# Attention with a bias: scores in three PSUM places of two banks instead of two places of three

## The chip, the cores and the metric

The kernel runs on one core of one Trainium2 chip. The time is the device time of one execution in microseconds (us); shorter is better. A core has five engines that run side by side, each through its own list of instructions: TensorE (PE; its weight loads are shown apart as PEld), VectorE (DVE), ScalarE (ACT), GpSimd (POOL) and SyncE (SP, which only issues transfers here). PSUM, which PE writes its products to, has eight banks of 512 fp32 values for each of 128 partitions. "One bank" below means a block of 128 x 512 scores.

## The reference

```python
batch, n_heads, seq_len, head_dim = 4, 8, 1024, 64
scale = 1.0 / np.sqrt(head_dim)
scores = scale * np.matmul(q, k.transpose(0, 1, 3, 2)) + bias      # bias: 1 x 1 x 1024 x 1024
scores_max = np.max(scores, axis=-1, keepdims=True)
attn = np.exp(scores - scores_max) / (np.sum(np.exp(scores - scores_max), axis=-1, keepdims=True) + 1e-8)
return np.matmul(attn, v)
```

There are 32 heads. The scores of a head are 1024 x 1024: with 128 keys on the partitions that is 16 banks, 512 banks in all.

## The kernel before

**The computation.** Two heads make a pair, 16 pairs. Scores are computed transposed: keys on the partitions, queries along the columns, in eight blocks of 128 keys and eight chunks of 128 queries. ACT takes the exponential from PSUM into a ring `E` of bf16 banks in SBUF (`s_exp`, L204); no maximum is subtracted. A second product of exp(scores) with V, which has a column of ones beside its 64 (`av_blocks`, L265; four matmuls of 65 columns for each bank), collects output and sum for a unit; DVE takes the reciprocal of the sum (`rs`, L276), multiplies (`ob`, L277), and SP stores.

**Running differences.** The bias is added to a place in PSUM only once for a set of chunks. When the next head comes to the same place, its scores are not written anew. Instead one matmul over 128 rows adds the new head's product and subtracts the old one's, since K of both heads stands on the two halves of the rows (`KA` for the second head of a pair, `KB` for the first head with the pair before it) and Q stands beside it with signs (`QA`, `QB`). Bias plus scores is thus kept up to date in PSUM. A step that begins a set anew is a *restart*: it writes the bias (four matmuls with `btraw` a bank) and then the head's scores.

**The places.** Six PSUM banks hold scores, `XY` = two places `sx` and `sy` of three banks (L79). The other two, tags `xa` and `xb`, serve in turn for transpositions (`px`) and for the accumulators of units (`po`). The eight chunks are divided into sets: A (chunks 6 and 7), B (3 to 5) and C (0 to 2). In A each place holds one chunk in two banks, in B and C each holds half the key blocks of three chunks in three banks. A *slot* is one filling of a place: `s_fill(s)` writes it (L151), slots alternate between the places, and slot s may be filled when ACT has read slot s-2. There are 192.

**The order.** Groups of pairs (L83): pairs 0 to 3 run through A, B, C; 4 to 8 through C, A, B; 9 to 15 through B, C, A. A set that goes on from one group to the next is not restarted. Where A goes over into a three-bank set, the third bank is filled early (`pre_slots`, `pe_pre`). K and Q of a pair are loaded by POOL, transposed by PE (L140), and copied by DVE (L763, L770) and by SP's transfers into a ring of RP = 9 pairs.

**DVE's share.** DVE computes some banks' exponentials itself with seven instructions, a *chain*: `d_fixed` reads the bank (L216), `d_steps` are L228 to L233. `mark_next` chooses the last bank of a slot for it, if DVE's queue of chain work is at most REM.

**The planner.** When the kernel is built, a planner walks through an estimated time line and writes out the order of each engine's instructions: it holds estimated costs (`EXP`, `E2P`, ...), times at which data are there (`R`, `raw_at`, `v_ready`), and picks for PE among a fill, a transposition (`pe_piece`) and AV work (`pe_av`). A fill goes as soon as its place is free; other work is taken if it ends before the fill is due, or if more than RING = 38 banks of E wait for AV. Loads are paced by `gate`, in slots. `cut_of` says which slots' exponentials are cut in two, so that a place comes free bank by bank.

**The prologue** (L289 to L487) is written out by hand: the first six slots (0 to 5), pairs 0 and 1, with loads as fp32 into the unused end of E and casts by DVE, ACT and POOL.

**The end.** The last pair's unit is divided into its two heads (`units`, L237).

Of the kernel before, what the change touches and what calls it, by code (L numbers as in the profile page):

```python
# [8 lines left out]
F32 = mybir.dt.float32  # L9
# [7 lines left out]
def kernel(  # L17
# [25 lines left out]
    RP = 9  # L43
    EB = 56
# [39 lines left out]
    steps = []  # L84
    prev = None
    for prs, ps_order in groups:
        for pa in ps_order:
            for pr in prs:
                for h in range(2):
                    restart = pr == prs[0] and h == 0 and pa != prev  # L90
                    steps.append((pa, pr, h, restart))
            prev = pa
    first_of = {}
    for pa, pr, h, restart in steps:
        first_of[pa, pr] = restart or first_of.get((pa, pr), False)
    NSTEP = len(steps)
    NS = 2 * NSTEP
    first_step = {}
    last_step = {}
    for i, (pa, pr, h, r) in enumerate(steps):  # L100
        first_step.setdefault(pr, i)
        last_step[pr] = i

    def pieces_of(pa, y):

        c0, W = CH[pa]
        if W == 2:
            return [(kc, c0 + y, 1, kc * P) for kc in range(NCH)]
        out_ = []
        for kk in range(4):  # L110
            col, ci, n = kk * W * P, 0, W
            while n:
                m = min(n, 4 - col // P % 4)
                out_.append((4 * y + kk, c0 + ci, m, col))
                col, ci, n = col + m * P, ci + m, n - m
        return out_

    def blocks_of(pa, y):
        return [(kc, c + j, col + j * P) for kc, c, n, col in pieces_of(pa, y) for j in range(n)]

    def nbanks(pa):
        return CH[pa][1]
# [22 lines left out]
    pass_reads = {}  # L145
# [5 lines left out]
    def s_fill(s, banks, third=False):  # L151

        pa, pr, h, restart = steps[s // 2]
        ps_ = XY[s % 2]
        r = pr % RP
        ms = mm_of.setdefault(s, [])
        for b in banks:
            todo, bias_ = [], []
            for kc, c, n, col in pieces_of(pa, s % 2):
# [3 lines left out]
                o = ps_[:, col:col + n * P]  # L163
                if restart:

                    todo.append((o, (KB if pr else KA)[:, r, kcol], QB[:, r, qcol]))
                    for j in range(n):
                        t = btraw[:, c + j, :].rearrange("p (kp kc) -> p kc kp", kc=NCH)[:, kc, :]
                        bias_.append((ps_[:, col + j * P:col + j * P + P], t, ident8[:]))
# [5 lines left out]
            for i, (o, lhsT, rhs) in enumerate(todo):  # L175
                m = nc.tensor.matmul(o, lhsT, rhs, start=restart and i == 0, stop=i == len(todo) - 1 or not restart,  # L176
                                     skip_group_check=True)
                for lo, hi, x in pass_reads.get(s % 2, []) if third else reads_of.get(s - 2, []):
                    if not lo <= b < hi:
                        apart(m, x)  # L180
                ms.append((b, m))

    def read_of(s, lo, hi, inst):
# [7 lines left out]
        if steps[s // 2][0] == "A":  # L191
            pass_reads.setdefault(s % 2, []).append((lo, hi, inst))
            for s2 in (x for x in mm_of if x > s and x % 2 == s % 2):
                for b, m in mm_of[s2]:
                    if not lo <= b < hi:
                        apart(inst, m)
        else:
            pass_reads.pop(s % 2, None)
# [3 lines left out]
    def s_exp(s, lo, hi):  # L202
        at = (e_pos[s] + lo) * 512
        x = nc.scalar.activation(E[:, at:at + (hi - lo) * 512], XY[s % 2][:, lo * 512:hi * 512], ACTF.Exp, scale=scale)  # L204
# [10 lines left out]
    def d_fixed(ch, s, b):  # L215
        i = nc.vector.tensor_scalar(ys[ch % 2].bitcast(I32), XY[s % 2][:, b * 512:(b + 1) * 512],  # L216
# [21 lines left out]
    for i, (pa, pr, h, r) in enumerate(steps):  # L238
        if h == 0:
            units += [(pa, pr, i, [0, 1])] if i < NSTEP - 2 else [(pa, pr, i, [0]), (pa, pr, i, [1])]  # L240
    NU = len(units)
    po = {}
    left = {u: 2 * 4 * CH[x[0]][1] * len(x[3]) for u, x in enumerate(units)}
# [8 lines left out]
    def av_blocks(u, s, b, tag):  # L252
        pa, pr, i0, hs = units[u]
        h = s // 2 - i0
        c0, W = CH[pa]
# [5 lines left out]
        for kc, c, col in blocks_of(pa, s % 2):  # L261
# [7 lines left out]
    def evac(u):  # L269
        pa, pr, i0, hs = units[u]  # L270
        c0, W = CH[pa]
# [9 lines left out]
    with tc.manual_schedule():  # L281
# [33 lines left out]
        for prs, po_ in groups:  # L315
            for pa in po_:
                if first_of[pa, prs[0]]:
                    c0, W = CH[pa]
                    g.memset(QB[D:, prs[0] % RP, c0 * P:(c0 + W) * P], 0.0)
# [19 lines left out]

        cast(g, btraw[:, 6, 5 * P:], sc[6][:, 5 * P:])  # L340
        for pr in (2, 3):
            if pr == 3:
                cast(g, kr1[:, 1].rearrange("p c d -> p (c d)"), sk1[:, 512:])
                load_q(pr, 6, 8)
            x = g.dma_start(out=raws[pr, 1].rearrange("p t c d -> p t (c d)"), in_=kf[pr])
            if pr == 2:
                after(x, behind)
            if pr == 2:
# [669 lines left out]
```

## Time and profile before

| | us |
|---|---|
| median of three runs (239.46 to 239.92) | 239.59 |
| the profiled execution | 239.7 |
| its span, first to last instruction | 237.8 |
| ACT busy, 275 instructions | 225.6 |
| PE busy, 4010 matmuls | 224.2 |
| PE weight loads busy | 187.7 |
| DVE busy, 461 instructions | 220.8 |
| POOL busy | 57.5 |
| first exponential starts | 7.23 |
| last exponential ends | 232.44 |

The profile is of one execution on the chip. It lists each instruction with engine, line of the kernel, what it writes and reads ("E<-sx" writes E from sx), start and length. Busy time is time in which at least one instruction of the engine runs; matmuls are pipelined and their ends are modelled, so that a busy PE need not be a PE at its peak. Exponentials overlap with the one before by 0.1 to 0.2 us, so that the distance from start to start is their real cost.

### The profile page before, as it was taken

The page shows a single profiled execution, that of the slowest core. Times are in us where ns is not written, and L with a number is a line of the kernel's source. Part 1 is how long each engine was busy: PE and PEld are TensorE (multiplying, and loading weights), DVE is VectorE, ACT ScalarE, POOL GpSimd, SP SyncE. Part 2 cuts the span into 40 slices and gives each one's busy share as a digit, 9 for nine tenths or more (in the row PEclk, how much of TensorE's full clock was granted, in tenths as well). Part 3 has the DMA queues.
Part 4 walks back from the last instruction along what each step waited for, and adds up shares of the span by engine and source line. Part 5 has one row for each costly group of instructions (what it writes and reads, how often), then busy time and mean ns, then how long its engine had stood idle before and what let it go on. Part 6 is the DMA issues. An engine that isn't in the chain of part 4 may idle for free.

```text
span 237.8 us, 9441 instructions
## 1 busy us (share of the span) xinstructions
PE 224.2 (94%) x4010; PEld 187.7 (79%) x4010; DVE 220.8 (93%) x461; ACT 225.6 (95%) x275; POOL 57.5 (24%) x82
## 2 busy tenths in 40 slices
PE   7999899999999999999999999999998989989892
PEld 3778788887888889987777888888887777888782
DVE  3686999999989999999999999999999999999993
ACT  4799999999999999999999999999999999999991
POOL 5695502544112224633220332000000000000000
PEclk9999999999999999999999999999999999999999
DMA  7899999999999649999998899312121111111012
GB/s 231 224 136 182 177 195 222 178 189 193 221 211 158 116 93 197 158 183 160 207 209 234 144 135 147 88 44 68 36 69 36 36 34 36 36 55 36 25 48 66
DMA packets 60633, 30.98 MB, mean 130 GB/s; under 512 B 36016, under 2 KB 56624, under 8 KB 60592
## 3 DMA queue, kind: packets, MB, share of 16 engines
q0 software_dynamic: 42272, 13.50, 55.2%
q1 hardware_dynamic: 18176, 16.62, 24.9%
q8 instruction: 31, 0.51, 0.9%
q10 hardware_dynamic: 144, 0.26, 0.5%
q14 instruction: 10, 0.08, 0.1%
HBM read 29.36 MB, written 8.39 MB: 159 GB/s over the span
## 4 chain that ended last, share of the span: by engine, by line
DVE 49%; PE 34%; ACT 7%; issue 7%; DMA 2%; ACTq 0%; DVEq 0%
PE sx L176 9%; PE po L265 8%; PE sy L176 8%; ACT E L204 7%; DVE scr L216 7%; DVE scr L232 7%; DVE e L233 6%; DVE ob L277 6%; DVE scr L231 5%; DVE scr L230 4%; DVE scr L229 4%; PE px L140 4%; DVE scr L228 3%; DVE QA L770 2%; DVE rs L276 2%
## 5 line engine op out<-in xcount | busy, mean ns | idle before, releaser
L204 ACT ACTIVATE E<-sy 128x512 bf16<-128x512 f32 (+2 forms) x151 | 127.9, 906 | 0.2
L204 ACT ACTIVATE E<-sx 128x1024 bf16<-128x1024 f32 (+2 forms) x110 | 115.2, 1065 | 1.5 <-PE sx L176 0.9
L265 PE MATMUL po<-VV,E 128*128 128x65 bf16 x1888 | 84.2, 194 | 2.1 <-DVE ob L277 1.1
L265 PEld LDWEIGHTS <-E 128*128 128x128 bf16 x1888 | 76.0, 98 | 10.3 <-DVE ob L277 2.4
L176 PEld LDWEIGHTS <-KA 128*128 128x128 bf16 x648 | 47.3, 98 | 11.6 <-issue 3.5
L176 PEld LDWEIGHTS <-KB 128*128 128x128 bf16 x600 | 44.0, 98 | 11.7 <-issue 4.6
L134 POOL DMA_DIRECT2D VV<-in_v_dram x32 | 28.8, 905 | 40.9 <-ACT E L204 37.2
L176 PE MATMUL sx<-QA,KA 128*128 128x128 bf16 (+2 forms) x312 | 36.1, 252 | 1.9 <-ACT E L204 1.6
L176 PE MATMUL sx<-QB,KB 128*128 128x128 bf16 (+2 forms) x300 | 35.5, 251 | 2.4 <-ACT E L204 1.7
L176 PE MATMUL sy<-QA,KA 128*128 128x128 bf16 (+2 forms) x312 | 36.0, 252 | 0.4 <-ACT E L204 0.2
L176 PE MATMUL sy<-QB,KB 128*128 128x128 bf16 (+2 forms) x300 | 35.4, 251 | 0.8 <-ACT E L204 0.3
L233 DVE SCALAR_TENSOR_TENSOR e<-scr 128x512 bf16<-128x512 f32 x40 | 27.6, 690 | 1.1
L232 DVE SCALAR_TENSOR_TENSOR scr<-scr 128x512 f32<-128x512 f32 x40 | 27.4, 684 | 0.0
L230 DVE SCALAR_TENSOR_TENSOR scr<-scr 128x512 f32<-128x512 f32 x40 | 27.3, 684 | 0.0
L231 DVE SCALAR_TENSOR_TENSOR scr<-scr 128x512 f32<-128x512 f32 x40 | 27.3, 683 | 0.0
L277 DVE TENSOR_TENSOR ob<-po,rs 128x384 f32<-128x384 f32 (+2 forms) x49 | 24.8, 506 | 2.0 <-DMA out_dram<-ob 0.4
L216 DVE TENSOR_SCALAR scr<-sx 128x512 int32<-128x512 f32 x32 | 21.9, 684 | 1.7 <-ACT E L204 1.5
L131 POOL DMA_DIRECT2D kr<-in_k_dram x12 | 8.5, 705 | 42.2 <-ACT E L204 35.1
L229 DVE TENSOR_SCALAR scr<-scr 128x512 int16<-128x512 int16 x40 | 17.2, 429 | 0.0
L228 DVE TENSOR_SCALAR scr<-scr 128x512 f32<-128x512 uint16 x40 | 17.0, 425 | 0.2
L176 PEld LDWEIGHTS <-btraw 128*128 128x128 bf16 x128 | 11.3, 148 | 1.2 <-issue 0.5
L770 DVE TENSOR_SCALAR QA<-px,sgn 128x1024 bf16<-128x1024 bf16 (+2 forms) x18 | 12.0, 666 | 0.0
(79 smaller groups left out, 167.9 us busy)
## 6 DMA issues: line engine op xcount, KB each, us to landing
out_dram<-ob SPq DMA_DIRECT2D x32, 192.0 KB, 2.8
VV<-in_v_dram POOLq DMA_DIRECT2D x32, 128.0 KB, 7.4
kr<-in_k_dram POOLq DMA_DIRECT2D x14, 256.0 KB, 5.4
KB<-KA SPq DMA_DIRECT2D x24, 128.0 KB, 4.4
qr<-in_q_dram POOLq DMA_DIRECT2D x12, 256.0 KB, 6.7
QB<-qn SPq DMA_DIRECT2D x22, 128.0 KB, 5.8
out_dram<-ob SPq DMA_DIRECT2D x15, 128.0 KB, 4.7
btraw<-in_bias_dram POOLq DMA_DIRECT2D x2, 768.0 KB, 9.0
```

What stands on the lines that cost most here:

```text
L134: return [nc.gpsimd.dma_start(out=VV[:, pr % RP, t * NCH:(t + 1) * NCH, :D], in_=vf[pr][:, t].rearrange("p (c d) -> p c d", d=D)) for t in ...
L176: m = nc.tensor.matmul(o, lhsT, rhs, start=restart and i == 0, stop=i == len(todo) - 1 or not restart, skip_group_check=True)
L204: x = nc.scalar.activation(E[:, at:at + (hi - lo) * 512], XY[s % 2][:, lo * 512:hi * 512], ACTF.Exp, scale=scale)
L216: i = nc.vector.tensor_scalar(ys[ch % 2].bitcast(I32), XY[s % 2][:, b * 512:(b + 1) * 512], scale * LOG2E * 65536.0, 127.0 * 65536.0, op0= ...
L228: (340, lambda: v_.tensor_scalar(sf, lo, G / 65536.0, None, op0=ALU.mult)),
L229: (340, lambda: v_.tensor_scalar(sp, hi, 0.0, 128.0, op0=ALU.max, op1=ALU.mult)),
L230: (600, lambda: v_.scalar_tensor_tensor(sb, sf, U2, sf, op0=ALU.add, op1=ALU.mult)),
L231: (600, lambda: v_.scalar_tensor_tensor(y, sf, U1, sf, op0=ALU.add, op1=ALU.mult)),
L232: (600, lambda: v_.scalar_tensor_tensor(sb, sb, V2, sp.bitcast(BF), op0=ALU.add, op1=ALU.mult)),
L233: (650, lambda: v_.scalar_tensor_tensor(e[:], y, V1, sb, op0=ALU.add, op1=ALU.mult)),
L265: nc.tensor.matmul(po[u][:, h - hs[0], c - c0, :], e_block(s, col), VV[:, pr % RP, h * NCH + kc, :], start=first, stop=left[u] == 0, skip_ ...
L277: nc.vector.tensor_tensor(ob[:], acc[:, :, :, :D], rs[:].to_broadcast([P, nh, W, D]), op=ALU.mult)
```

## The change

Six banks are still used for scores, now as three places `z0`, `z1`, `z2` of two banks. Every slot has two banks, and there are 256. Slot s waits for the slot that last used its place, `was[s]`, in the steady part slot s-3.

In B and C the 24 blocks of a head (8 key blocks x 3 chunks) go over the three places in order, eight to each. Set A is divided into A0 (chunk 6) and A1 (chunk 7). For the first group the slots 0 to 15 use `z0` for A0 and `z1` for A1, and `z2` only in the prologue. In the later groups, now pairs 4 to 9 and 10 to 15, set A runs over three places (`pass_a`): of the twelve heads, `z0` and `z1` take A0 and A1 of the first eight, while `z2` takes A0 of the last four and then A1 of these.

A unit is now a pair with a range of chunks; where a pair's A0 and A1 run at different times (pairs 8, 9, 14, 15), each chunk is a unit of its own, and the last six slots are divided by head, the last three by chunk too. RP goes from 9 to 10, E from 56 to 50 banks, RING from 38 to 36, REM from 5000 to 3500. The early fill of a third bank is dropped, as are most cuts. `mark_next` may choose slots that follow each other, and always bank 1 of the next slot to be filled.

In the prologue the transposed K lies in `z2`; DVE copies both halves of KA (ACT did one); POOL casts pair 1's q (DVE did); the second half of K is copied by ACT and DVE (DVE alone did); pair 1's q is transposed earlier; K of pair 3 is loaded behind q of pair 3.

```diff
-    RP = 9
-    EB = 56
+    RP = 10
+    EB = 50
...
-    XY = [ps.tile([P, 3 * 512], F32, tag=t, name=t) for t in ("sx", "sy")]
-    CH = {"A": (6, 2), "B": (3, 3), "C": (0, 3)}
-    groups = [(range(0, 4), "ABC"), (range(4, 9), "CAB"), (range(9, NP), "BCA")]
+    Z = [ps.tile([P, 2 * 512], F32, tag=t, name=t) for t in ("z0", "z1", "z2")]
+    CH = {"A0": (6, 1), "A1": (7, 1), "B": (3, 3), "C": (0, 3)}
...
+        if W == 1:
+            return [(kc, c0, kc * P) for kc in range(NCH)]
+        return [(i // W, c0 + i % W, i % 8 * P) for i in range(8 * y, 8 * y + 8)]
...
+    slots = [(y, "A%d" % y, 0, pr, h) for pr in range(4) for h in range(2) for y in range(2)]
+    NA = len(slots)
+    def pass_(pa, prs):
+        return [(y, pa, y, pr, h) for pr in prs for h in range(2) for y in (2, 0, 1)]
+    def pass_a(prs):
+        hd = [(pr, h) for pr in prs for h in range(2)]
+        out_ = []
+        for i in range(8):
+            out_ += [(2, "A%d" % (i // 4), 0) + hd[8 + i % 4], (0, "A0", 0) + hd[i], (1, "A1", 0) + hd[i]]
+        return out_
+    g0, g1, g2 = range(4), range(4, 10), range(10, NP)
+    slots += pass_("B", g0) + pass_("C", g0) + pass_("C", g1) + pass_a(g1) + pass_("B", g1)
+    slots += pass_("B", g2) + pass_("C", g2) + pass_a(g2)
+    for s, (y, pa, yb, pr, h) in enumerate(slots):
+        was.append(at_.get(y))
+        at_[y] = s
+        b = slots[was[s]] if was[s] is not None else None
+        restart.append(b is None or b[1:3] != (pa, yb) or 2 * b[3] + b[4] + 1 != 2 * pr + h)
...
+    for s, (y, pa, yb, pr, h) in enumerate(slots):
+        joint = pa in "BC" or (pr - g1[0]) % 6 < 4 or pr < 4
+        hs, c = [0, 1], (CH[pa] if pa in "BC" or not joint else (6, 2))
+        if s >= NS - 6:
+            hs = [h]
+            if s >= NS - 3:
+                c = CH[pa]
...
+        cast(g, *q_part(1, 6, 8, sq1))
...
-        on(0, 2, 3, nc.scalar.copy(KA[:D, 0, :HK], pk[0][:D]))
-        on(1, 2, 3, v_.tensor_copy(KA[:D, 0, HK:], pk[1][:D]))
+        on(2, 0, 1, v_.tensor_copy(KA[:D, 0, :HK], pk[0][:D]))
         v_.tensor_copy(QB[:D, 0, 6 * P:], pq_[:D].rearrange("p c q -> p (c q)"))
+        on(2, 1, 2, v_.tensor_copy(KA[:D, 0, HK:], pk[1][:D]))
...
+        nc.scalar.copy(KA[D:, 0, :HK], pk0[0][D:])
+        v_.tensor_copy(KA[D:, 0, HK:], pk0[1][D:])
...
-        DMIN, DTAIL, DMAL, RING, PSL, PSU, URG, NEAR, REM = 14, 8, 5200, 38, 60, 150, 24, 3, 5000
-        G0, G1, G2, G3, G4, G5 = 18, 5, 12, 56, 6, 8
+        DMIN, DTAIL, DMAL, RING, PSL, PSU, URG, NEAR, REM = 14, 9, 5200, 36, 100, 200, 20, 3, 3500
+        G0, G1, G2, G3, G4, G5 = 20, 7, 16, 78, 10, 8
...
         def cut_of(s):
-            n = nbanks(steps[s // 2][0])
-            if s in mark or s < 6:
-                return None
-            if n == 3 and s // 2 + 1 in restarts:
-                return 2
-            if n == 2 and s % 2:
-                return 1
-            if s - 1 in mark or (n == 2 and s + 1 in mark):
-                return n - 1
-            return None
+            return s not in mark and (s < NA and s % 2 == 1 or s == NS - 1)
...
-            if s in pre_slots or s != len(fill_end) or not DMIN <= s < NS - DTAIL or s - 1 in mark or len(open_ch) >= 3 \
-                    or len(ch_run) >= 2 or ch_left[0] > REM:
+            if s != len(fill_end) or not DMIN <= s < NS - DTAIL or len(open_ch) >= 3 or len(ch_run) >= 2 or ch_left[0] > REM:
                 return
...
-            if s >= NS or s - 2 >= len(act_end) or (s - 2 in mark and len(read_end[s - 2]) < nbanks(steps[s // 2 - 1][0])):
+            if s >= NS or was[s] >= len(act_end) or (was[s] in mark and len(read_end[was[s]]) < 2):
                 return None
```

More of the change, by code (lines that the diff above doesn't have):

```diff
@@ L149, in apart, with s_fill @@
             tc.declare_no_dep(later.ins, earlier.ins, reason="different banks of one slot")
-    def s_fill(s, banks, third=False):
-        pa, pr, h, restart = steps[s // 2]
-        ps_ = XY[s % 2]
+    def s_fill(s):
+        y, pa, yb, pr, h = slots[s]
         r = pr % RP
         ms = mm_of.setdefault(s, [])
-        for b in banks:
+        for b in range(2):
             todo, bias_ = [], []
-            for kc, c, n, col in pieces_of(pa, s % 2):
+            for kc, c, n, col in pieces_of(pa, yb):
                 if col // 512 != b:
@@ L175, in s_fill @@
             for i, (o, lhsT, rhs) in enumerate(todo):
-                m = nc.tensor.matmul(o, lhsT, rhs, start=restart and i == 0, stop=i == len(todo) - 1 or not restart,
+                m = nc.tensor.matmul(o, lhsT, rhs, start=restart[s] and i == 0, stop=i == len(todo) - 1 or not restart[s],
                                      skip_group_check=True)
-                for lo, hi, x in pass_reads.get(s % 2, []) if third else reads_of.get(s - 2, []):
+                for lo, hi, x in reads_of.get(was[s], []):
                     if not lo <= b < hi:
@@ L510 @@
         next_load = next_v = 4
-        restarts = [i for i in range(1, NSTEP) if steps[i][3]]
-        pre_slots = []
-        for i in restarts:
-            if steps[i - 1][0] == "A":
-                pre_slots += [2 * i, 2 * i + 1]
-        pre_done = {}
         dve_q = []
@@ L695, in loads @@
             while next_v < NP and s > gate(next_v, 1) \
-                    and not any(units[u][1] == next_v - RP for u in range(av_u, NU)):
+                    and not any(units[u][0] == next_v - RP for u in range(av_u, NU)):
                 for x in load_v(next_v):
```

350 lines of the change are left out of this document (140 added, 210 removed).

## The prediction

> **What bounds the kernel now.** I read the page's parts 1 and 2, then busy time by stage, then ACT's own groups by form and its timeline, then PE's.
>
> ```profile
> span 237.8 us, 9441 instructions
> ...
> PE 224.2 (94%) x4010; PEld 187.7 (79%) x4010; DVE 220.8 (93%) x461; ACT 225.6 (95%) x275; POOL 57.5 (24%) x82
> ...
> PEclk9999999999999999999999999999999999999999
> ```
>
> Three engines lie within two per cent of each other and TensorE's clock is granted in full, so no single share of busy time decides. The windows say which engine is full in which stage (columns: length; then PE, PEld, DVE, ACT, POOL busy):
>
> ```profile
> 16.00:30.00 14.00, 12.54 (x202) 10.45 (x198) 12.01 (x26) 13.78 (x22) 8.69 (x11) 1.00 1.73 181
> 30.00:80.00 50.00, 49.79 (x924) 41.35 (x924) 48.36 (x98) 49.46 (x49) 16.20 (x21) 1.00 1.28 190
> 80.00:110.00 30.00, 29.34 (x602) 26.85 (x601) 29.38 (x62) 29.77 (x43) 12.78 (x17) 1.00 1.21 157
> 110.00:150.00 40.00, 39.99 (x727) 32.09 (x726) 39.24 (x81) 39.77 (x41) 8.47 (x10) 1.00 1.05 176
> 150.00:232.00 82.00, 76.42 (x1367) 65.57 (x1364) 80.80 (x166) 81.79 (x107) 0.00 (x0) 1.00 0.15 45
> ```
>
> ACT is busy 98 to 99.7% from 16 us to the last exponential. But its instructions overlap, so that column hides short waits; the starts show them:
>
> ```profile
> 24.38 0.75 ACT L204 ACTIVATE E<-sx 128x512 bf16<-128x512 f32 x1
> 24.86 0.77 ACT L204 ACTIVATE E<-sy 128x512 bf16<-128x512 f32 x1
> 25.33 1.21 ACT L204 ACTIVATE E<-sx 128x1024 bf16<-128x1024 f32 x1
> 26.24 1.22 ACT L204 ACTIVATE E<-sy 128x1024 bf16<-128x1024 f32 x1
> ...
> 35.27 1.47 ACT L204 ACTIVATE E<-sx 128x1536 bf16<-128x1536 f32 x1
> 36.66 1.45 ACT L204 ACTIVATE E<-sy 128x1536 bf16<-128x1536 f32 x1
> 38.01 1.45 ACT L204 ACTIVATE E<-sx 128x1536 bf16<-128x1536 f32 x1
> 39.34 1.03 ACT L204 ACTIVATE E<-sy 128x1024 bf16<-128x1024 f32 x1
> ```
>
> From start to start, the undisturbed steps (tenth percentile of all starts) are 0.476 us for one bank, 0.903 for two, 1.330 for three: 0.427 a bank and 0.049 an instruction. The trace has 122, 91 and 56 of these (the last has no follower): 121 x 0.476 + 91 x 0.903 + 56 x 1.330 = 214.3 us. From the first exponential (7.23) to the start of the last (231.75) are 224.5 us. Less one cast between them (1.0), that leaves **9.2 us in which ACT did not run at its rate**. By stage: 1.64 before 16 us, then 0.73, 2.06, 1.33, 1.31 and 2.19 in the five windows. Of these 0.92 are steps of 17 ns (0.920 for 0.903), the rest waits of 0.06 to 0.52 us.
>
> Can they go? That depends on PE. I give each matmul its median step: 29.5 ns for 65 columns, 55.5, 108.5 and 162 for 128, 256 and 384, 58 for a bias block, 36 for a transposition. What is then left of PE's time is 2.67 us in 30:80, of which 2.41 are the changes between transpositions and other matmuls (23 of some 0.1 us, none of them touched). In 110:150 it is 2.51, with 2.52 such. So **PE is full in 30:80 and 110:150** and ACT's 3.37 us there are mostly PE's. In 80:110 PE has 2.3 us beside these changes, in 150:232 about 12. Counting exponentials against the 65-column matmuls that use them (four a bank), 30 to 38 banks wait for AV from 50 to 75 us, 10 at 90, 39 at 135, 2 to 3 from 165 on: work is put off up to the limit RING=38 in both full stretches.
>
> **The change, part by part.** The sum is made against the profiled execution, 239.7 us (span 237.8 and 1.9 around it); the median of the three runs, 239.59, is 0.1 lower.
>
> 1. *Three places.* A fill may start once the exponential three slots back is done, no longer two back. Before, with 128x1536, a fill has 1.33 us of the other place's exponential for 0.66 of matmuls and the hand-overs; after it has 2 x 0.90 for 0.45. What goes: in 80:110 the 1.33 less 0.15 of small steps, 1.18; in 150:232 2.19 - 0.28 = 1.91 (the larger waits there, 1.0 us in sum, sit where DVE reads its bank late, 209.4 to 212.5 and near 220; one place more covers such a reading); in 110:150 only the waits before 130 us, when AV can still be put off, 0.49; in 30:80 no more than the 0.26 that PE has left; in 16:30 0.15, as its 0.52 at 29.1 is PE waiting for DVE's copies (L773). Together **-4.0**. The lower end is 0 (a later wait takes each place), the upper 6.7 (all that are not small steps).
> 2. *Form of the exponentials.* 256 slots of two banks. With 40 DVE banks as now: 206 x 0.903 + 60 x 0.476 (40 marked; 20 from the ten slots cut in two) = 214.6, against 214.3: **+0.3**. Not fewer instructions: 266 against 269. But 206 two-bank steps stand where 91 were, and these show 0.903 and 0.920 about equally often, the three-bank ones nearly always 1.330: 115 x 0.008 = **+0.9**, between 0 and 2.6 (all at 0.920, less what is paid now).
> 3. *More restarts.* The third place restarts twice in each later two-chunk stage: 20 slots of two banks instead of 32 banks, so 32 bias matmuls more, 32 x 0.058 = 1.9 us of PE, half in each of the stages now at 90:110 and 210:232. PE's idle time there hides them, **0**; without it +1.9.
> 4. *Outputs.* Units rise from 49 to 55: the pairs in the third place are divided by chunk. One evacuation's fixed part is 0.17 (L276) + 0.16 (L277: 558, 424, 292 ns for 384, 256, 128 columns, so 0.16 at none): 6 x 0.33 = 2.0 us on DVE, which is 97 to 99% full from 30 to 232. A chain is 3.73 us by its own starts, so half a chain less, half a bank more on ACT: **+0.2** (0 to +0.4). A kernel shorter by 2 us gives DVE half a chain less again: **+0.2**. One chain more or less is 0.43 us, from the DVE limit REM (5000 to 3500).
> 5. *Ring of E, 56 to 50 banks, limit 38 to 36.* In the full stretches two banks less can be put off: 2 x 4 x 0.0295 = 0.24 us of PE each; I take one: **+0.25** (0 to 0.5). Ten pairs and groups of 4, 6, 6: the transpositions are the same in number, six pairs' before the second group's end instead of five, the rest due later (slot 160 of 256, before 108 of 192). One pair is 1.35 us of PE and lands where AV backlog falls (75:90): **0**.
> 6. *Prologue.* KA's first half goes from ACT to DVE and QB's copy between the halves: the first scores waited 0.48 us for QB (6.20), and start about 0.3 earlier. That is lost at once, since the second half of K waits for its DMA until 7.11 in both. The transposition of pair 1's q moves ahead of slot 3's bias (4 matmuls and two changes): slot 3's exponential +0.15. On POOL one cast of 128x256 is added (0.5 for 128x384, so about 0.4) and K of pair 3 goes behind its q: all later POOL loads shift 0.4 us. The bias of stage B landed at 21.6 and is first used at 23.71, so that is hidden; uncovered it would be +0.4. Two more memsets lie in POOL's 1.75 us wait. **+0.15** (-0.3 to +0.5).
> 7. *Tail.* From the last exponential's end, 232.44, to 237.8 are 5.35 us: 36 AV matmuls with 0.25 of wait for an accumulator, two small evacuations with a 0.40 wait for an output buffer, the store. The last unit becomes one chunk of one head; but five units end in the last six slots instead of two. **-0.2** (-0.8 to +0.8).
>
> Sum: -4.0 + 0.3 + 0.9 + 0.2 + 0.2 + 0.25 + 0.15 - 0.2 = -2.2, **237.5 us** from 239.7, and 237.4 on the median's scale; I say 237.5.
>
> **A rule against this reading.** The Trainium skill (Perfetto Trace Analysis, Identifying the Most-Contended Engine) calls matmul busy time a bad measure of headroom and takes the share of weight loads. By it PE would have 17% free in 30:80 (41.35 of 50), and the stalls there could go too, which is rival B. My reading rests on steps between starts, not on the busy column; no run here has yet shown which holds.
>
> **Rivals.**
> - *B, PE can be packed further.* For: weight loads leave gaps of 0.1 us and more at each hand-over. Against: 0.26 us are left in 30:80 by the steps. Then 2.06 - 0.24 - 0.26 = 1.56 and 1.31 - 0.14 - 0.49 = 0.68 go as well: 237.5 - 2.2 = **235.3**.
> - *C, the place does not do what it says:* the planner gives the time won to AV, and the waits come back as waits for E's ring or for DVE's late bank. For: 39 banks wait at 135. Against: from 150 us no more than 5 wait. **239.6**, within 0.5.
> - *D, slower: the two accumulators.* In the last 24 slots, units of two pairs run side by side and hold both accumulators; both end together in each of four rounds, and AV stands until DVE has finished a chain step (0.69) and a first evacuation (0.6), 1.3 us. For: the trace has waits for ob up to 0.6 us with units one after another. Against: fills (2.7 us a round) can go meanwhile. PE's spare time in 22 us at the end is 22 x 12/82 = 3.3, less 1.0 of bias: 2.3. With nothing beside it 4 x 1.3 = 5.2, so 2.9 us of AV are left after the last exponential: 237.5 + 2.9 = **240.4**. It makes the kernel slower once a round stands more than (2.3 + 2.1) / 4 = 1.1 us.
>
> **How the numbers follow.** Forecast 0.47 (its own range by the unknown terms 236.3 to 239.0), B 0.20, C 0.11, D 0.22. The measurement tells 0.2%, 0.5 us, from no change: forecast and B are faster (0.67), C is the same (0.11), D slower (0.22). The range from 235.0 to 240.5 leaves out the upper half of D and the lower end of B.
>
> **What would show it.** Step 1: ACT's excess over its steps near 5 us, with hardly any in the last third, and over 1.5 us still in 30:80. Step 2: two-bank steps between 0.903 and 0.920. Step 4: 38 to 40 chains, 55 reciprocals. Step 6: slot 3 not over 0.3 later. D would show as PE waiting for ob in the last 25 us and a tail over 7 us; B as ACT's excess under 3 us. I am wrong if AV backlog is at its limit over more of the span than now, or if a pair's loads are late.

## The result and the profile after

The changed kernel takes 236.75 us, the median of five runs (236.56 to 237.96), against 239.79 for the kernel before on the same occasion (239.46 to 240.59): a ratio of 0.9888, 95% interval 0.9853 to 0.9924. That is 3.0 us less; 237.5 was forecast, 2.2 less than the profiled execution.

The page of the changed kernel, the lines that answer to those of before:

```profile
span 234.6 us, 9577 instructions
...
PE 223.7 (95%) x4042; PEld 189.0 (81%) x4042; DVE 218.5 (93%) x466; ACT 224.4 (96%) x272; POOL 57.3 (24%) x85
...
PEclk9999999999999999999999999999999999999999
```

PE has 32 matmuls more and the same clock; nothing else on these lines shows where 3 us went. By stage (length; PE, PEld, DVE, ACT, POOL busy):

```profile
16.00:30.00 14.00, 12.77 (x198) 10.69 (x198) 12.33 (x26) 13.64 (x21) 8.65 (x12) 1.00 1.67 180
30.00:80.00 50.00, 48.98 (x897) 39.80 (x894) 48.92 (x99) 49.49 (x58) 18.34 (x24) 1.00 1.58 196
80.00:110.00 30.00, 29.61 (x625) 27.46 (x622) 29.52 (x61) 29.76 (x37) 10.82 (x14) 1.00 1.10 161
110.00:150.00 40.00, 39.18 (x735) 33.54 (x733) 39.20 (x86) 39.67 (x48) 8.12 (x10) 1.00 0.87 142
150.00:230.00 80.00, 77.68 (x1421) 66.56 (x1420) 78.51 (x167) 80.00 (x96) 0.00 (x0) 1.00 0.20 58
```

ACT is as full as before in every stage, so its busy column can't tell the two apart. The starts of the exponentials can. ACT's groups by form show what it runs now (count, then busy and mean ns):

```profile
L209 ACT ACTIVATE E<-z 128x1024 bf16<-128x1024 f32 x207 | 199.4, 1142 | 1.6 <-PE z L189 1.3 <-ACT E L209 0.2
L209 ACT ACTIVATE E<-z 128x512 bf16<-128x512 f32 x51 | 35.2, 724 | 0.0
L426 ACT ACTIVATE E<-z 128x512 bf16<-128x512 f32 x8 | 4.2, 598 | 1.2 <-PE z L422 0.8 <-PE z L413 0.4
```

With the steps of the prediction, 207 x 0.903 + 58 x 0.476 = 214.5 us (the last exponential, a single bank, has no follower), against 214.3 before. So the whole span of the profiled pair divides thus (us; "casts and copies" reaches from the start of the first cast or copy among the exponentials to the next exponential, and in the kernel before 0.39 of its 1.01 is waiting):

| | before | after | difference |
|---|---|---|---|
| first exponential starts | 7.23 | 7.03 | -0.20 |
| ACT at its steps | 214.25 | 214.53 | +0.28 |
| casts and copies between | 1.01 | 1.25 | +0.24 |
| ACT's waits (starts over steps) | 9.26 | 7.21 | -2.05 |
| start of the last exponential to the end | 6.03 | 4.59 | -1.44 |
| span | 237.79 | 234.62 | -3.17 |

The waits by stage (to 16, to 30, 80, 110, 150 us, rest) were 1.64, 0.73, 2.06, 1.33, 1.31, 2.19 and are 1.08, 0.87, 1.59, 1.07, 1.27, 1.33. DVE computes 39 chains instead of 40, and 55 units are put out:

```profile
L238 DVE SCALAR_TENSOR_TENSOR e<-scr 128x512 bf16<-128x512 f32 x39 | 26.9, 690 | 1.0
L290 DVE RECIPROCAL rs<-po 128x6 f32<-128x6 f32 (+3 forms) x55 | 9.9, 180 | 0.4
```

Two theories of the waits were then open. *Theory 1*, of the prediction: waits in 30:80 and 110:150 are PE's, which is full. *Theory 2*: the waits of before are the hand-over between two places, and those of after come from PE's written order. Beside the places stood three rivals for the gain: the planner's new limits, the new prologue, the finer units at the end.

### The profile page after: what moved, and what is told of

Same layout as the page of the kernel before. It is cut to its first block, busy times and chain, and to the rows that moved or that the text cites. A ratio compares the mean times of both kernels' runs of the same rounds, so it can differ in the third digit from the quotient of the medians.

```text
span 234.6 us, 9577 instructions
## 1 busy us (share of the span) xinstructions
PE 223.7 (95%) x4042; PEld 189.0 (81%) x4042; DVE 218.5 (93%) x466; ACT 224.4 (96%) x272; POOL 57.3 (24%) x85
## 4 chain that ended last, share of the span: by engine, by line
PE 46%; DVE 42%; issue 7%; ACT 3%; DMA 1%; DVEq 0%; ACTq 0%
PE z L189 24%; PE po L280 14%; DVE scr L221 6%; DVE ob L291 5%; DVE e L238 5%; DVE scr L237 5%; DVE scr L236 5%; DVE scr L235 4%; PE px L155 4%; ACT E L209 3%; DVE scr L234 3%; DVE scr L233 3%; DVE QA L736 2%; DVE rs L290 2%; DVE KA L729 2%
## 5 line engine op out<-in xcount | busy, mean ns | idle before, releaser
L209 ACT ACTIVATE E<-z 128x1024 bf16<-128x1024 f32 (+1 forms) x258 | 216.4, 1059 | 1.6 <-PE z L189 1.3
L280 PE MATMUL po<-VV,E 128*128 128x65 bf16 x1892 | 87.5, 194 | 2.5 <-DVE KA L729 0.8
L189 PE MATMUL z<-QA,KA 128*128 128x128 bf16 (+2 forms) x624 | 73.7, 252 | 2.3 <-ACT E L209 1.7
L189 PE MATMUL z<-QB,KB 128*128 128x128 bf16 (+2 forms) x600 | 73.5, 251 | 1.5 <-ACT E L209 0.9
L149 POOL DMA_DIRECT2D VV<-in_v_dram x32 | 28.4, 890 | 38.9 <-ACT E L209 34.3
L291 DVE TENSOR_TENSOR ob<-po,rs 128x384 f32<-128x384 f32 (+3 forms) x55 | 25.7, 468 | 2.5 <-DMA out_dram<-ob 0.7
L221 DVE TENSOR_SCALAR scr<-z 128x512 int32<-128x512 f32 x39 | 26.6, 683 | 1.4 <-PE z L189 1.2
L189 PE MATMUL z<-ident,btraw 128*128 128x128 bf16 x160 | 16.6, 227 | 0.0
L189 PEld LDWEIGHTS <-btraw 128*128 128x128 bf16 x160 | 14.4, 148 | 0.6
L280 PE MATMUL po<-VV,e 128*128 128x65 bf16 x156 | 11.2, 194 | 0.0
L155 PE MATMUL px<-ident,qr 128*64 128x128 bf16 x256 | 11.1, 223 | 0.0
```

What stands on the lines that cost most here:

```text
L149: return [nc.gpsimd.dma_start(out=VV[:, pr % RP, t * NCH:(t + 1) * NCH, :D], in_=vf[pr][:, t].rearrange("p (c d) -> p c d", d=D)) for t in ...
L189: m = nc.tensor.matmul(o, lhsT, rhs, start=restart[s] and i == 0, stop=i == len(todo) - 1 or not restart[s], skip_group_check=True)
L209: x = nc.scalar.activation(E[:, at:at + (hi - lo) * 512], Z[slots[s][0]][:, lo * 512:hi * 512], ACTF.Exp, scale=scale)
L221: i = nc.vector.tensor_scalar(ys[ch % 2].bitcast(I32), Z[slots[s][0]][:, b * 512:(b + 1) * 512], scale * LOG2E * 65536.0, 127.0 * 65536.0, ...
L280: nc.tensor.matmul(po[u][:, h - hs[0], c - c0, :], e_block(s, col), VV[:, pr % RP, h * NCH + kc, :], start=first, stop=left[u] == 0, skip_ ...
L291: nc.vector.tensor_tensor(ob[:], acc[:, :, :, :D], rs[:].to_broadcast([P, nh, W, D]), op=ALU.mult)
```

## The experiments

Times are medians; a ratio is to the kernel before on the same chip. "Waits" are ACT's starts over its steps, as above.

**e1, a third place in name only.** From slot 16 on a fill also waits for the exponential two slots back, in the planner and on the chip.

```diff
+                if s >= NA and i == 0:
+                    for lo, hi, x in reads_of.get(s - 2, []):
+                        if lo <= b < hi:
+                            after(m, x)
...
+            if s >= NA and (s - 2 >= len(act_end) or (s - 2 in mark and len(read_end[s - 2]) < 2)):
+                return None
...
-            ready = max([o + SEM] + [read_end[was[s]].get(b, 0) + E2P - b * cost for b in range(2)])
+            back = s - 2 if s >= NA else was[s]
+            ready = max([o + SEM] + [read_end[back].get(b, 0) + E2P - b * cost for b in range(2)])
```

> The changed kernel, but from slot 16 on a fill also waits for the exponential two slots back, as with two places; everything else stays. Theory (the third place pays for two-bank slots): exponential end to fill start 0.3, fill 0.45, to the exponential 0.26, in sum 1.0 us against 0.90 us of the exponential between, so 0.1 us of stall in most of 200 unmarked slots and more after a marked one (0.48): 10 to 25 us longer, 247 to 262 us, the excess of ACT's starts over its steps above 15 us. Rival (the gain comes from the forms of the slots and the planner's limits, the place is idle): within 0.5 us of the changed kernel.

Measured: 269.81 us, ratio 1.126 (1.1236 to 1.1283), waits 44.7 us. The rival, that the third place is idle, falls. The time is 8 us above the top of the expected range, and the waits do not lie where the expectation put them: of 43.2 us after 17 us, 23.7 follow the 56 exponentials of one bank (0.41 us at the median), mostly slots of which DVE took the other bank; behind the 196 of two banks the median wait is 0.02 us, not 0.1, and the other 19.5 us stand in fewer, longer waits. What follows is limited: slots of two banks cannot do without the third place, above all where DVE takes a bank. It doesn't compare them with two places of three banks.

**e2, the planner's limits alone,** in the kernel before.

```diff
-    EB = 56
+    EB = 50
...
-        DMIN, DTAIL, DMAL, RING, PSL, PSU, URG, NEAR, REM = 14, 8, 5200, 38, 60, 150, 24, 3, 5000
+        DMIN, DTAIL, DMAL, RING, PSL, PSU, URG, NEAR, REM = 14, 8, 5200, 36, 100, 200, 20, 3, 3500
```

> The kernel before with the changed kernel's limits alone: E of 50 banks, RING 36, PSL 100, PSU 200, URG 20, REM 3500. Theory (the places and the end make the gain): the limits alone give nothing, 239.2 to 240.5 us. Rival (the new limits of the planner make the gain): 236.5 to 238 us.

Measured: 239.71 us, ratio 1.0002 (0.9985 to 1.0019). The limits alone make no difference in the kernel before. Its profile is of use beyond that, as a second look at the old places: waits 11.2 us and 4.01 us from the end of the last exponential to the end of the span, where the kernel before had 9.3 and 5.35 in the same total time. The tail of before holds AV work. Its last row of AV starts after the last exponential has ended (232.44); the last row of the changed kernel starts before its last exponential ends (230.87), and 4 matmuls are left then, as in e2:

```profile
232.62 1.32 PE L265 MATMUL po<-VV,E 128*128 128x65 bf16 x32 [0.25 <-DVE ob L277]
```

```profile
229.66 1.56 PE L280 MATMUL po<-VV,E 128*128 128x65 bf16 x24 [0.17 <-DVE ob L291]
```

So the longer tail of before need not be a cost of its own: where the order leaves AV for the end, ACT has waited less before it. I take waits and tail together: 14.6 and 15.2 us with two places, 7.21 + 3.75 = 11.0 after.

**e3, the end undivided.**

```diff
-        if s >= NS - 6:
+        if s >= NS:
```

> The changed kernel without its division of the last units by head and chunk: the last pairs' units stay whole as in the steady part. Theory (the shorter tail comes from the smaller last units): from the end of the last exponential to the end of the span 4.3 to 5.0 us instead of 3.7, 0.6 to 1.3 us slower. Rival (the tail is shorter because hardly any AV work is left at the last exponential, 2 banks at 230 us against 11 before): within 0.3 us of the changed kernel, the AV matmuls after the last exponential few as now.

Measured: 236.80 us (236.61 to 236.91), ratio 0.9879 (0.9865 to 0.9892), no different from the changed kernel. From the last exponential's end to the end are 4.11 us instead of 3.75, but that exponential ends 0.27 earlier, since ACT waits 1.16 us in 30:80 instead of 1.59. PE's matmuls stand in the same order in both kernels, and the last units can't reach that stage, so this difference does not come from them. The finer units shorten the tail by 0.4 in this pair of profiles, and the medians do not show it; they are not the gain.

**e4, no bank for DVE at restarts.**

```diff
-            if s != len(fill_end) or not DMIN <= s < NS - DTAIL or len(open_ch) >= 3 or len(ch_run) >= 2 or ch_left[0] > REM:
+            if any(restart[x] for x in range(s, min(s + 3, NS))) or s != len(fill_end) or not DMIN <= s < NS - DTAIL or len(open_ch) >= 3 or len(ch_run) >= 2 or ch_left[0] > REM:
```

> The changed kernel, but DVE takes no bank of a slot that is a restart or comes up to two slots ahead of one. Theory (what is left of ACT's waits, 0.3 to 0.7 us each near 25, 93, 115, 180 and 208 us, comes from restarts, whose fill of 0.93 us is longer than a marked slot's exponential of 0.48): 1 to 2 of 7.2 us of excess go, at the price of no or one chain: 0.5 to 1.5 us faster. Rival (PE's total work sets these stretches): the waits move to the slots behind, within 0.4 us.

Measured: 237.37 us (236.50 to 238.23), ratio 0.9904 (0.9880 to 0.9928). Waits fall from 7.21 to 5.66: in 16:30 from 0.87 to 0.05, in 80:110 and 110:150 from 1.07 and 1.27 to 0.50 and 0.52. The waits of 0.06 us or more at restarts fall from 1.7 to 0.1, as theory had it. But in 30:80 the waits rise from 1.59 to 2.51, and 37 chains instead of 39 leave 2 x 0.43 us more to ACT. The restarts together with DVE's banks are a cause; nothing is gained.

**e5 and e6, half of the AV product left out,** in both kernels: the test of theory 1. Shown is e5's edit; in e6 only the count of a unit's blocks, `left`, is written otherwise.

```diff
-    left = {u: 2 * 4 * CH[x[0]][1] * len(x[3]) for u, x in enumerate(units)}
+    left = {u: 4 * CH[x[0]][1] * len(x[3]) for u, x in enumerate(units)}
...
-            if col // 512 != b:
+            if col // 512 != b or kc % 2:
                 continue
...
-            return ready, 122, emit
+            return ready, 61, emit
```

> The kernel before with every second matmul of the AV product left out (odd key blocks; the planner counts 61 ns instead of 122 for a bank), so PE has 30 us less to do and the output lacks half of V. Theory (PE is full from 30 to 80 and from 110 to 150 us, so ACT's waits there are PE's): the excess of ACT's starts over its steps, 3.4 us in these two stretches, falls under 1.2 us, and the kernel is 2 to 4 us shorter. Rival (these waits are the hand-over between two places): at least 2.5 us of the 3.4 stay.

> The same, in the changed kernel: every second AV matmul left out. Theory (PE full in 30:80, restarts elsewhere): excess in 30:80 from 1.6 to under 0.5 us, the waits at restarts (24, 93, 115, 180, 208 us) stay at 0.3 us or more each, the whole about 1.5 to 2.5 us shorter than the changed kernel. Rival (hand-over or DVE's late bank): the excess in 30:80 stays over 1.2 us. If the two places of before cost something of their own, this kernel has at least 1 us less excess than the kernel before with half its AV.

Measured, one execution each: 239.52 and 238.83 us (spans 237.7 and 235.7). The kernel before with half its AV, by stage in 30 to 150 us:

```profile
30.00:80.00 50.00, 44.46 (x691) 34.32 (x686) 48.14 (x98) 48.40 (x48) 15.35 (x20) 1.00 1.30 192
80.00:110.00 30.00, 25.98 (x439) 21.75 (x439) 29.48 (x61) 29.35 (x45) 13.88 (x18) 1.00 1.19 165
110.00:150.00 40.00, 36.69 (x576) 27.95 (x573) 39.45 (x81) 39.91 (x42) 8.28 (x10) 1.00 1.05 169
```

PE issues 233 matmuls fewer in 30:80 and its weight loads are busy 34.3 instead of 41.4 us, yet ACT waits 3.13 us there (2.06 with all of AV), and 10.5 in all. The changed kernel without half its AV waits 2.83 in 30:80 and 8.7 in all. **Theory 1 falls:** by the prediction's own steps 233 AV matmuls are 6.9 us, a seventh of PE's work in 30:80, and PE has 9.9 us left there instead of 2.7; the waits stay. PE was full because the planner puts AV wherever there is room, not because the work had to be done then. The difference in waits between the two kernels stays too (10.5 and 8.7). But e5 does not show what took the place of theory 1: its order of PE is a new one, and most of its waits are of another kind than those of before (below).

**e7 and e8, the limit of AV put off,** 24 and 44 banks instead of 36.

```diff
-        DMIN, DTAIL, DMAL, RING, PSL, PSU, URG, NEAR, REM = 14, 9, 5200, 36, 100, 200, 20, 3, 3500
+        DMIN, DTAIL, DMAL, RING, PSL, PSU, URG, NEAR, REM = 14, 9, 5200, 24, 100, 200, 20, 3, 3500
```

> The changed kernel with the limit of AV work put off at 24 banks instead of 36. Theory (PE is full up to 85 us and only putting off AV keeps ACT going): 12 banks x 4 x 29.5 ns = 1.4 us less can be put off, 0.9 to 1.6 us slower, the excess in 30:80 up by about that. Rival (the ring is not the limit): within 0.3 us.

> The same limit at 44 banks (E has 50). Theory: 8 banks more can be put off, 0.9 us of PE: 0.4 to 1.0 us faster, excess in 30:80 from 1.6 to under 1.0. Rival (E's 50 banks are full before the limit counts: 44 wait at 85 us already, and ACT then waits for E instead): within 0.3 us, or slower.

Measured: 238.16 us (236.62 to 238.29), ratio 0.9917 (0.9892 to 0.9942), and 237.07 us (236.86 to 239.38), ratio 0.9905 (0.9874 to 0.9937). These are no tests of the limit: built with 24 or with 44, the program is that of the changed kernel, byte for byte. At none of the three values does RING decide what the planner picks, and in all three profiles up to 45 banks wait for AV.

They are of use as ten more executions of the changed kernel. All fifteen have a median of 237.18 us (236.56 to 239.38), so that the gain is rather 2.5 us than 3.0. The three profiles of this one program also tell chance from cause. Waits from 16 us on are 6.13, 6.10 and 6.19 us, and 1.59, 1.55 and 1.66 in 30:80. But slot 6 begins at 14.96, 15.74 and 15.43. And the time is longer than the span by 1.93 to 2.82 us in these fifteen, by 1.76 to 1.99 in the kernel before beside e1 to e11; no view shows what lies outside the span.

**Where the waits come from, by the traces.** For each wait of 0.06 us or more after 16 us I took the fill that the exponential waited for, and when its place had last been read. In the kernel before these waits sum up to 6.3 us: 3.0 to 3.4, by where the line is drawn, have a fill that begins some 0.35 us or less behind ACT's read of the place (hand-over), 1.6 to 1.8 are behind DVE's read of its bank, and in the other 1.1 to 1.7 the fill comes later than that. In e5 the same count gives 1.1, 1.4 and 5.0. A hand-over in the timeline of before:

```profile
75.95 1.48 ACT L204 ACTIVATE E<-sy 128x1536 bf16<-128x1536 f32 x1
...
77.08 0.78 PE L265 MATMUL po<-VV,E 128*128 128x65 bf16 x20
...
77.29 1.05 ACT L204 ACTIVATE E<-sx 128x1024 bf16<-128x1024 f32 x1
77.70 0.82 PE L176 MATMUL sy<-QB,KB 128*128 128x384 bf16 x6
...
78.39 1.02 ACT L204 ACTIVATE E<-sy 128x1024 bf16<-128x1024 f32 x1
```

`sy` is read until 77.43; its fill begins 0.27 later and begins its last matmul at 78.19; the exponential starts 0.2 after that. DVE has taken one bank of `sx`, so ACT's own work there is two banks, 0.90 us, and the chain takes 1.10: 0.2 us late, even with the fill at once. With three banks on ACT (1.33 us) the chain would be in time.

In the changed kernel the waits from slot 17 on sum up to 4.8 us, none behind DVE's read. 1.7 are at restarts; of the rest all but 0.2 have a fill that begins 0.59 to 1.20 us after its place was free. In two of these PE itself stood idle first: ahead of slot 122 (0.66 us, the longest) for 0.75 us, as AV in front of the fill waited for DVE's copy of KA, and ahead of slot 71 (0.23 us) for 0.39. DVE's banks still play a part: 13 of the 19 waits follow a slot of which DVE had taken a bank, so that ACT was done with it after 0.48 us. One of them, slot 35:

```profile
38.34 2.50 ACT L209 ACTIVATE E<-z 128x1024 bf16<-128x1024 f32 x3
41.11 1.02 ACT L209 ACTIVATE E<-z 128x1024 bf16<-128x1024 f32 x1 [0.28 <-PE z L189]
```

```profile
39.48 0.60 PE L189 MATMUL z<-QB,KB 128*128 128x256 bf16 x4
39.92 0.29 PE L280 MATMUL po<-VV,E 128*128 128x65 bf16 x4
40.05 0.28 PE L280 MATMUL po<-VV,e 128*128 128x65 bf16 x4
40.17 0.41 PE L280 MATMUL po<-VV,E 128*128 128x65 bf16 x8
40.42 0.60 PE L189 MATMUL z<-QB,KB 128*128 128x384 bf16 x4
```

The first exponential of the merged row had read the place by 39.43, so the fill of slot 35 could have followed the one at 39.48. The written order has 16 AV matmuls first, and the fill starts at 40.42. The third exponential of the row, at 40.16, has one bank only, as DVE took the other; ACT is done with it after 0.48 us and waits until 41.11.

**e9 and e10, fills earlier in PE's order,** e10 with DVE's banks kept from restarts as well (the first of the two changes is e10's alone).

```diff
-            if s != len(fill_end) or not DMIN <= s < NS - DTAIL or len(open_ch) >= 3 or len(ch_run) >= 2 or ch_left[0] > REM:
+            if any(restart[s:s + 2]) or s != len(fill_end) or not DMIN <= s < NS - DTAIL or len(open_ch) >= 3 or len(ch_run) >= 2 or ch_left[0] > REM:
...
-            ready = max([o + SEM] + [read_end[was[s]].get(b, 0) + E2P - b * cost for b in range(2)])
+            ready = max([o + SEM] + [read_end[was[s]].get(b, 0) + E2P - 400 - b * cost for b in range(2)])
```

> The changed kernel, but the planner counts a place as free 0.4 us earlier when it puts a fill into PE's order (fills then stand before AV and transpositions that it put ahead of them). Theory (what is left of ACT's waits is PE's written order: fills begin 0.6 to 1.0 us after their place is free, behind AV or a transposition, mostly after a slot whose second bank is DVE's): of the 5 us of waits after 16 us at least 2 go, 1.0 to 2.5 us faster than the changed kernel. Rival (PE cannot do more: a fill that comes earlier makes AV late, E's ring or the accumulators then hold ACT): waits of the same sum at other slots, within 0.4 us; or slower, if PE now stands at the fills.

> The same, and DVE takes no bank of a slot that is a restart or comes just before one. Theory (the other waits are at restarts, whose fill of 0.93 us is longer than the exponential of a slot with DVE's bank, 0.48): another 0.5 to 1.0 us of waits go at 16:30, 90:100 and 180, no or one chain less: 0 to 0.8 us faster than with early fills alone. Rival: the chain lost costs as much (0.43 us): within 0.3 us.

Measured: e9 238.98 us (238.02 to 241.57), ratio 0.9967 (0.9942 to 0.9993), waits 8.7 us: slower than the changed kernel, though time outside the span, 2.1 to 3.4 us, has a share in it. e10 237.52 us (236.78 to 238.19), ratio 0.9899 (0.9873 to 0.9926), waits 6.7 us, 38 chains: no better. The waits moved to other slots, and outside the restarts their fills again begin 0.3 to 1.5 us after the place is free. One constant of the planner does not cure the order. That the order causes the waits of after is thus read from the traces, and not shown by an experiment that removes them. The changed kernel without DVE's banks was not run.

**e11, three steps of the prologue in the kernel before:** DVE copies both halves of KA with QB's copy between them, K's second half is transposed ahead of the second fill's bias, POOL casts pair 1's q.

```diff
+                cast(g, *q_part(1, 6, 8, sq1))
...
-        on(0, 2, 3, nc.scalar.copy(KA[:D, 0, :HK], pk[0][:D]))
+        on(0, 2, 3, v_.tensor_copy(KA[:D, 0, :HK], pk[0][:D]))
+        v_.tensor_copy(QB[:D, 0, 6 * P:], pq_[:D].rearrange("p c q -> p (c q)"))
         on(1, 2, 3, v_.tensor_copy(KA[:D, 0, HK:], pk[1][:D]))
-        v_.tensor_copy(QB[:D, 0, 6 * P:], pq_[:D].rearrange("p c q -> p (c q)"))
...
-        first, last = fresh()
-        for b in range(2):
-            bias_(0, b, 6, b)
...
+        first, last = fresh()
+        for b in range(2):
+            bias_(0, b, 6, b)
...
-        cast(v_, *q_part(1, 6, 8, sq1))
```

> The kernel before with three steps of the changed prologue: DVE copies both halves of KA with QB's copy between, K's second half is transposed ahead of the second fill's bias, POOL casts pair 1's q. Theory (the new order of the prologue brings 0.3 to 0.5 us of the gain): slot 6's exponential begins at 15.0 to 15.2 us instead of 15.4 to 15.5, the kernel is 0.2 to 0.5 us faster than before. Rival (its start follows the landing of K's second half, 6.1 to 7.2 us by chance): slot 6 at 15.2 to 15.5 and within 0.2 us.

Measured: 239.92 us, ratio 1.0001 (0.9987 to 1.0016), slot 6 at 15.42 us. These steps alone bring nothing. The whole new prologue may: in the profiles slot 6 begins at 15.37 to 15.70 with two places (five of them, mean 15.50) and at 14.83 to 15.74 with three (nine, mean 15.16). The landing of K's second half, by chance early or late, explains part of the spread. Where it lands by 6.51 us, slot 6 begins at 15.37 and 15.51 with two places and at 14.83 to 15.23 with three (six profiles, mean 15.01); where it lands from 6.85 on, the means are 15.53 and 15.45. So the new prologue seems to make use of an early landing, worth 0.3 to 0.5 us then; no run has it by itself.

**e12, two places without DVE's chains.**

```diff
-        DMIN, DTAIL, DMAL, RING, PSL, PSU, URG, NEAR, REM = 14, 8, 5200, 38, 60, 150, 24, 3, 5000
+        DMIN, DTAIL, DMAL, RING, PSL, PSU, URG, NEAR, REM = 999, 8, 5200, 38, 60, 150, 24, 3, 5000
```

> The kernel before without DVE's share of the exponentials: ACT computes all 512 banks, so its steps grow by 40 x 0.427 = 17.1 us and the kernel to 250 to 256 us. Theory (the waits of the two places come with DVE's banks: after ACT's two of three banks, 0.90 us, the fill of the other place, 0.4 to its start, 0.5, 0.2 to the exponential, is 0.2 us late, and places stay blocked until DVE has read; with three banks on ACT, 1.33 us, it is in time): ACT's excess after 16 us falls from 7.6 to under 3 us, and waits at three-bank slots are rare outside restarts. Rival (the waits are PE's written order, whatever ACT's share): the excess after 16 us stays over 5 us.

Measured, one execution: 257.5 us; waits 13.4 us, 11.3 of them after 16 us. The waits after 16 us did not fall under 3 us, as theory expected, and by the number the rival's sign (over 5 us) is there. A new cause has the largest part: 5.0 us fall between 60 and 70 us, where the transpositions of pairs 6 and 7 stand in PE's order ahead of fills and wait for their loads. PE's rows there:

```profile
60.27 0.49 PE L176 MATMUL sx<-QB,KB 128*128 128x256 bf16 x3
...
62.74 0.64 PE L140 MATMUL px<-ident,qr 128*64 128x128 bf16 x16 [1.98 <-DMA qr<-in_q_dram]
```

Nor did the waits fall before that: they are 1.79 us in 16:30 (0.73 in the kernel before) and 2.04 in 30:60 (1.40), and in 30:60 the fills begin 0.4 to 0.9 us after ACT's read, so the order of PE has its part there, as the rival says. From 80 us on, where loads do not interfere, 0.30, 0.59 and 1.35 us are left of 1.33, 1.31 and 2.19, and of the three-bank slots outside the restarts a single one waits 0.06 us or more (0.07). There the hand-over of before thus needs DVE's banks, as theory 2 says, unless it is the longer kernel, which gives PE some 18 us more in all; e12 can't part the two. For the time before 80 us theory 2 rests on the traces.

## Why the prediction came out right, and which of its steps did not

The time lay in the range and nearer to the forecast (237.5) than to any rival; the median of all fifteen executions of this program, 237.18, is nearer still. But the sum holds several terms that were wrong and cancel: -4.0 for the places came out at -1.49 after 16 us, +0.9 and +0.25 at nothing, the prologue's +0.15 at -0.52 in the profiled pair and the tail's -0.2 at -1.6. That they add up to so near the time is luck.

1. *Three places, -4.0.* Measured -2.05 in all, -1.49 after 16 us: -0.47 in 30:80 (-0.26 forecast), -0.26 in 80:110 (-1.18), -0.04 in 110:150 (-0.49), -0.86 after 150 (-1.91), +0.14 in 16:30 (-0.15). The step that failed is the sentence "PE is full in 30:80 and 110:150 and ACT's 3.37 us there are mostly PE's": e5 halves AV and the waits stay. What stood in its place, by the trace of before, was the hand-over of a place from ACT to PE and back (3.0 to 3.4 us) and DVE's late reading (1.6 to 1.8); in the trace of after hardly any of either is left (0.2 us). The second half of the failure is that waits at restarts (1.7 us) and behind PE's written order (3.0) took much of their place. Step 1 had this as its lower end, "a later wait takes each place", and only part of the way was gone.
2. *Form, +0.3 and +0.9.* The first is right (+0.28). The second is nothing: some 0.9 us were in small steps before and are now; of the 207 two-bank steps 160 are at most 0.905 and 33 near 0.920, not half and half.
3. *More restarts, 0.* The 32 bias matmuls themselves are hidden, but the restarts hold 1.7 us of waits of after: their fill takes 0.93 us, and e4 removes nearly all of these waits by keeping DVE from them. The term was put at nothing because PE has idle time there; what it left out is that a long fill comes late for a slot that ACT is done with in 0.48 us.
4. *Outputs and chains, +0.4.* 55 units and 39 chains, as forecast.
5. *Ring, +0.25.* Nothing can come from the limit, since values of 24 to 44 give the same program. That E has 50 banks instead of 56 was not tried alone in the changed kernel; in the kernel before, e2 has it at no cost.
6. *Prologue, +0.15.* In the profiled pair -0.52 at slot 6, -0.3 in the mean of all profiles. The claim that the early start "is lost at once", as K's second half lands at 7.11 in both, did not hold in this pair: it landed at 6.12 in the execution after. It does not land at a fixed time (below), and where it lands late, little of the early start is left (e11).
7. *Tail, -0.2.* Measured -1.6 from the last exponential's end (5.35 to 3.75). The prediction read 36 AV matmuls behind the last exponential's end in the kernel before; 32 start after it. e3 shows that the division does not make the gain, and e2 that two places can have 4.0 as well, with more waits before. Waits and tail together went down by 3.6 us in this pair, so what step 1 put into the waits alone came in part as a shorter tail, which it did not foresee.

**The rivals.** B, that PE has room, was right in its mechanism and wrong in its time: e5 shows the room, against my reading from the steps between starts. By the Trainium skill (Perfetto Trace Analysis, Identifying the Most-Contended Engine), PE's headroom is to be judged not by its busy time but by the share of its peak that its matmuls reach and by the share of weight loads. The latter is 83% in 30:80, and e5 agrees with that. The room did not bring B's 2.2 us; by the traces the written order takes it back. C, that waits come back elsewhere, is what happened to more than half of the gain of step 1, behind AV and transpositions in PE's order and at restarts rather than at E's ring. D did not occur: in the last 25 us the accumulators stop PE rarely, and the tail is 3.75 us.

**The signs.** ACT's excess is 7.2 us and not near 5, and 1.33 of it lie behind 150 us, where hardly any was to be; 1.59 in 30:80, 39 chains and 55 reciprocals are as said. The prediction named AV work at its limit over more of the span as a sign that it was wrong. It is: 36 us instead of 10. Yet it cost nothing that the traces show, and none of the three limits changes what the planner writes.

**What is shown of the cause.** The planner's limits (e2) and the units at the end (e3) are excluded as the gain, the prologue has at most some 0.5 us of it, and e1 shows that the third place is needed. That the places make the rest is read from the traces of the waits and supported, not proved, by e12 from 80 us on. The new groups of pairs, the rule that DVE may take banks of slots that follow each other, the dropped cuts and the new pacing of loads came with the places and were not run by themselves. No kernel tried beats the changed one; e3 equals it.

## What to carry to other kernels

A full engine is no bound if a planner fills its gaps: take half of its work away and see whether the others' waits go. Where two engines hand a buffer to and fro, add up the chain from the last read to the next use (here the read ends 0.14 us after the other exponential starts, 0.27 more to the fill, 0.5 to its last matmul, 0.2 to the exponential: 1.10) and set it against the shortest work the other buffer gives (0.90 once a bank is taken away), not against the usual (1.33). A third buffer removes that wait only as far as the written order lets the refill go first. Before a knob's runs are compared, see whether the program changed at all: here 24, 36 and 44 gave the same one, and its medians still lay 1.4 us apart.

## What the runs showed of the hardware that was not expected

- In the traces of before and after, matmuls of 128 columns, each with its weight load, go by at 56 ns from start to start at the median, and those of 65 columns at 29.5; a change between transpositions (128 x 64 blocks) and other matmuls costs 92 ns one way and 115 the other.
- Four loads issued on one queue at the same times (the one of K's second half at 1.76 us) land from run to run at different times: that half at 6.12 to 7.77 us in the fourteen profiles, and at 6.12, 7.77 and 7.48 in the three of one program. One profile tells the start of this kernel to no better than some 0.8 us (slot 6 at 14.96 to 15.74 in these three).
- An ACT instruction overlaps the one before it, so a wait of up to 0.15 us leaves no idle time in its row; the kernel before had 3.4 us of idle time before its exponentials in the profile's groups (1.7 of it in the prologue) and 9.3 us of waits by the starts.
